# Retention of one mixer layer in two steps of four chunks instead of three steps of two

## The chip, the cores and the metric

The kernel runs on one core of one Trainium2 chip. The metric is the device time of one execution in microseconds (us). TensorE (PE in the profile) does the matrix products and writes them to PSUM; VectorE (DVE), ScalarE (ACT) and GpSimd (POOL) do the rest; SyncE (SP) only issues transfers.

## The reference, cut to what matters

The reference is a decoder trunk of two layers over 512 tokens of 1024 features. Each layer mixes with three parallel branches (RWKV-7, retention, a causal spatial gating unit, here "gating"), merges them with sigmoid gates, and follows with a gated MLP. The change is about the second and the third branch and about the merge:

```python
def retention_branch(p, cos, sin):            # 4 heads, 4 chunks of 128 tokens
    ...
    scores = jnp.einsum('bhnid,bhnjd->bhnij', qc, kc) * decay_in[:, None]
    inner = jnp.einsum('bhnij,bhnje->bhnie', scores, vc)
    kv = jnp.einsum('bhnjd,bhnje,hj->nbhde', kc, vc, k_dec).astype(jnp.float32)
    def step(R, kv_n):
        return R * chunk_decay + kv_n, R
    _, R_prev = lax.scan(step, jnp.zeros(...), kv)
    cross = jnp.einsum('bhnid,nbhde,hi->bhnie', qc, R_prev, q_dec)
    y = (inner + cross).transpose(0, 2, 3, 1, 4).reshape(B, S, RET_HEADS, RET_V_DIM)
    y = y * lax.rsqrt(jnp.mean(y * y, axis=-1, keepdims=True) + EPS)
    return (y.reshape(B, S, RET_V_WIDTH) * jax.nn.silu(g)).astype(p.dtype)

def sgu_branch(p, ln_g, ln_b, w_s, b_s):
    ...
    mixed = jnp.einsum('gij,bnjgd->bnigd', w, vc) + b_s.T[:, :, None]
    return u * mixed.reshape(B, S, SG_WIDTH)

proj = jnp.einsum('bsgc,gcd->bsgd', branches, w_branch[l])
x = x + jnp.sum(gates * proj, axis=2) @ w_out[l]
```

For each chunk n retention needs the scores of the chunk, a sum over the chunk for the state (`kv`), and a read-out: scores times values, plus the queries times the state that the earlier chunks left.

## The kernel before, in words

All large products are done in two halves of float32r: an operand is split into a high part (`hi`, or `sh`/`wh` for weights) and a low part (`lo`, `sl`/`wl`), and `mm3` (lines 153 to 163) issues three matmuls of 128 x 512 for each 128 x 128 block of weights. Weights come in units of 128 x 512: SP loads one (`wr`), ACT casts its high part (line 140), DVE subtracts the low part (line 141). `unit` (line 95) prepares them up to three units ahead in this stage, and the parts lie in a ring of 16 buffers (`r`), which also holds the turned queries and keys (`qF`, four buffers), the decayed keys (`kd`, three) and gating's normalised values (`sgv`, four). A second ring (`u`) has 31 buffers; the normalised input `h` takes 16 of them until the last product that reads it, the values and the gate of retention take 8, and scores (`sc`), states (`R`) and read-outs (`ry`) come from it too.

PSUM has eight banks in two pools of four: `acc` (line 78), where the large products add up, and `sm` (line 81), for everything small. A bank is handed on when the engine that reads it is done.

The code is emitted in one order and a planner orders the instructions of each engine at build time: by emission, but an instruction that is not ready in the planner's reckoning lets later ones pass. An instruction under `keep_in_program_order` is held behind the instruction emitted just before it on its engine. All of retention's and gating's small matmuls are held so; the matmuls of a merge are not.

The second half of the mixer (lines 420 to 458) is driven by the string `SEQ` (line 29), one letter or digit for a step, once for each of the two layers:

- `0`, `2`, `1`: one of eight blocks of a merge with branch 0 (RWKV), 2 (gating), 1 (retention): `merge`, line 1067. Twelve matmuls on one unit of weights into one `acc` bank; POOL issues the load of the block's gate (`gth`, line 1071); DVE multiplies gate and product (line 1074), which frees the bank; for branch 2 POOL, for branch 1 DVE adds to the sum (line 1077), and after branch 1 the sum is split.
- `U`: one of gating's two remaining up-projections (24 matmuls, one `acc` bank, freed by DVE at line 1040).
- `H`: `ret_heads` (line 922) reorders queries and keys on ACT and makes `kd` on DVE.
- `G`: `sgu_out` (line 1055), one of gating's four blocks: four matmuls into one `sm` bank, DVE reads it at line 1061.
- `S`: `ret_pair` (line 940) with the chunks to read out, to score and to sum. Its matmuls are emitted in this order: scores times values, queries times states, keys times queries (new scores), keys times values (sums for the states). Then ACT copies the read-outs out of PSUM (line 972), DVE masks the scores (line 976) and runs the states (lines 984 and 986), and the read-outs are normalised (lines 991 to 999): square on ACT, sum on DVE, power on POOL (line 996), product with the gate on DVE (line 999).
- `Y`: `ret_out` (line 1001) transposes the gated read-outs and splits them for the merge.

Before, `S` runs three times: scores of chunks 0 and 1 with all three sums; read-out of 0 and 1 with scores of 2 and 3; read-out of 2 and 3. Every `S` takes two `sm` banks for two chunks of read-outs, two for two chunks of scores, and the first takes two more for the sums.

The small matmuls are in plain float32, and each of them stands as two instructions in the trace.

Of the kernel before, what the change touches and what calls it, by code (L numbers as in the profile page):

```python
# [13 lines left out]
ADD, SUB, MUL, POW, MAX = ALU.add, ALU.subtract, ALU.mult, ALU.pow, ALU.max  # L14
# [3 lines left out]
S = 512  # L18
NC = 4
# [6 lines left out]
KEPT = 6  # L26
PRE = {(0, "f", 2): 0, (0, "f", 4): 1, (0, "f", 6): 2, (0, "f", 8): 3, (0, "d", 0): 4, (0, "d", 1): 5, (0, "d", 2): 6, (0, "d", 3): 7,
       (0, "d", 4): 8, (0, "d", 5): 9, (0, "d", 6): 10}
SEQ = "0 H G G 0 S 0 U U S G 0 G 0 0 S 2 2 Y 0 0 2 1 2 1 2 1 2 1 2 1 2 1 1 1"
NRAW = 3  # L30
AHEAD = {None: 2, "p": 4, "r": 3, "f": 3, "u": 5, "q": 4}
DEEP = 6
# [20 lines left out]
class Emit:  # L53
# [357 lines left out]
    def mixer(self, l, nst):  # L411
        self.pool = None
        with self.tc.tile_pool(name=f"rw{l}", bufs=1) as rp:
            self.rwp = rp
            self.filler = self.fillers(l)
            st = self.rwkv(l, nst)
        for _ in self.filler:
            pass
        self.rp = self.tc.tile_pool(name=f"ff{l}", bufs=NFP)
        self.fp = self.rp.__enter__()  # L420
        self.gup, self.bs, self.ws = self.f(n="gup"), self.f((128, 4, 128), n="bs"), self.f((128, 4, 128), n="ws")
        with self.tc.high_priority():
            self.nc.sync.dma_start(self.gup, self.a["gup"][l])
        self.nc.sync.dma_start(self.bs.rearrange("p g i -> p (g i)"), self.a["sgb"][l:l + 1, :].to_broadcast([128, 512]))
        self.nc.sync.dma_start(self.ws, self.a["sgw"][l])
        self.pool = "f"
        sg, out = self.sgu_v(l), self.rwkv_out(l, *st)
        self.nc.vector.tensor_tensor(self.ws, self.ws, self.c("le").unsqueeze(1).to_broadcast([128, 4, 128]), op=MUL)
        self.qk = []
        for c in range(NC):  # L430
            self.qk.append(self.f(n="qkT"))
            self.turned(self.qk[c], self.f(n="qkt"), self.ro[c], self.nc.gpsimd)
        self.wsp = self.split(self.ws.rearrange("p g i -> p (g i)"), self.f)
        for step in (sg, sg, out, sg, out, sg, None, out, sg, out, sg):
            next(step) if step else self.sgu_bias()
        yrw, ysg, mg, out, m2 = self.yrw, [], [], [], 0
        self.pool = "r"
        rest = self.sgu_u(l, range(2, 4))
        rows = iter([((), (0, 1), (0, 1, 2)), ((0, 1), (2, 3)), ((2, 3),)])
        for step in SEQ.split():  # L440
            if step == "S":
                self.ret_pair(*next(rows))
            elif step == "G":
                ysg.append(self.sgu_out(len(ysg)))
            elif step == "H":
                self.ret_heads()
            elif step == "U":
                next(rest), next(rest)
            elif step == "Y":
                yret = self.ret_out()  # L450
            elif step == "0":
                mg.append(self.merge(l, 0, len(mg), yrw))
            elif step == "2":
                mg[m2] = self.merge(l, 2, m2, ysg, mg[m2])
                m2 += 1
            else:
                out.append(self.split(self.merge(l, 1, len(out), yret, mg[len(out)], self.nc.vector), self.f))
        return out
# [481 lines left out]
    def ret_pair(self, read=(), score=(), state=()):  # L940


        nc, V, A, T, po = self.nc, self.nc.vector, self.nc.scalar, self.nc.tensor, self.tc.keep_in_program_order
        hv, hd = [slice(0, 64), slice(64, 128)], [(j, h) for j in range(2) for h in range(2)]
        X, Z = [[self.sm((128, 2, 2, 128)) for _ in range(2)] if cs else None for cs in (read, score)]

        def mm(o, lhsT, rhs, start, stop=True):
            po(T.matmul(o, lhsT, rhs, start=start, stop=stop, skip_group_check=True))  # L948

        for k, c in enumerate(read):  # L950
            for j, h in hd:
                i = 2 * j + h
                mm(X[h][:, k, j, :], self.sc[c][:, j, h, :], self.vt[c][:, 128 * i:128 * i + 128], k == j == 0, c == 0)
        for k, c in enumerate(read):
            for j, h in hd if c else ():
                mm(X[h][:, k, j, :], self.qF[c][hv[h], j, :], self.R[c][hv[h], j, :], False)
        for k, c in enumerate(score):
            for j, h in hd:
                mm(Z[h][:, k, j, :], self.kF[c][hv[h], j, :], self.qF[c][hv[h], j, :], k == j == 0)
        pks = []  # L960
        for c in state:
            if c % 2 == 0:
                pks.append(self.sm((128, 2, 2, 128)))
            for j, h in hd:
                i = 2 * j + h
                mm(pks[-1][hv[h], c % 2, j, :], self.kd[c][:, i, :], self.vt[c][:, 128 * i:128 * i + 128], c % 2 == j == 0)
        rm = self.c("rmask").rearrange("p (j h i) -> p j h i", h=2, i=128)
        ys = []
        for k, c in enumerate(read):
            ys.append(self.u((128, 2, 2, 128), n="ry"))  # L970
            for h in range(2):
                A.copy(ys[k][:, :, h, :], X[h][:, k])
        for k, c in enumerate(score):
            sc = self.u((128, 2, 2, 128), n="sc")
            for h in range(2):
                V.tensor_tensor(sc[:, :, h, :], Z[h][:, k], rm[:, :, h, :], op=MUL)
            self.sc[c] = sc
        for c in state:
            if c % 2 == 0:
                Rs = self.u((128, 2, 2, 128), n="R")  # L980
            pk, R, Rn = pks[c // 2][:, c % 2], self.R.get(c), Rs[:, c % 2]
            for j in range(2):
                if c == 0:
                    V.tensor_copy(Rn[:, j, :], pk[:, j, :])
                else:
                    V.scalar_tensor_tensor(Rn[:, j, :], R[:, j, :], self.c("rdec")[:, j:j + 1], pk[:, j, :], op0=MUL, op1=ADD)
            self.R[c + 1] = Rn
        for k, c in enumerate(read):
            y, g = ys[k].rearrange("p j h e -> p (j h) e"), self.yg[c]
            sq = self.u((128, 4, 128), n="rsq")  # L990
            A.activation(sq, y, AF.Square)
            ss = self.small((128, 4), "rss")
            V.tensor_reduce(ss, sq, axis=AX.X, op=ADD)
            V.tensor_scalar(ss, ss, 4.0 / 128, 4e-6, op0=MUL, op1=ADD)
            rr = self.small((128, 4), "rrr")
            nc.gpsimd.tensor_tensor(rr, ss, self.c("mhalf")[:, 0:4], op=POW)
            for i in range(4):
                o = g[:, 128 * i:128 * i + 128]
                V.scalar_tensor_tensor(o, y[:, i, :], rr[:, i:i + 1], o, op0=MUL, op1=MUL)
# [482 lines left out]
```

## Time and profile before

| what | value |
|---|---|
| median of 3 runs | 1692.36 us (1691.71 to 1693.19) |
| the profiled execution | 1690.56 us |
| its span, first to last instruction | 1688.9 us |
| granted TensorE clock | 0.999 |
| DVE busy | 1216.6 us (72%) |
| ACT busy | 793.7 us (47%) |
| POOL busy | 261.2 us (15%) |
| moved by DMA | 260.01 MB, mean 154 GB/s |

The profile page gives the busy time of each engine, the chain of work that ended last, and groups of instructions by line. Times in the trace's views are us from the start of the span. A matmul's row lasts longer than the distance to the next one, since matmuls are pipelined, so what PE takes is read from the distance between starts, not from the durations. The stage of the change lies between about 358 and 458 us in layer 0 and 844 us later in layer 1.

### The profile page before, as it was taken

Reading aid. Unit: us, or ns where it says so; the run is one execution under the profiler, and the core shown is the slowest. Engines: PE = TensorE matmul, PEld = TensorE weight load, DVE = VectorE, ACT = ScalarE, POOL = GpSimd, SP = SyncE. Lnnn points to the kernel's source line nnn. Section 1 sums busy time; section 2 is a strip of 40 time slices with the busy share of each in tenths; the row PEclk is TensorE's granted clock in tenths of the full one; section 3 lists DMA queues with packets and bytes.
Section 4 is the critical chain, followed back from the end, with each engine's and each line's share of the span. In section 5 each row is a group of like instructions: output and inputs, shape, how many; then the busy total and the mean of one; then the engine's idle time right before and its main releaser. Section 6 shows DMA issues by size and latency. Waiting matters only on the chain.

```text
span 1688.9 us, 27943 instructions
## 1 busy us (share of the span) xinstructions
PE 1680.4 (100%) x10247; PEld 1382.5 (82%) x10247; DVE 1216.6 (72%) x2115; ACT 793.7 (47%) x1365; POOL 261.2 (15%) x376
## 2 busy tenths in 40 slices
PE   9999999999999999999999999999999999999998
PEld 7888877888888888888888888778888888888887
DVE  7888745578669887655568888455786688887777
ACT  6563543554255444433346544335542544444555
POOL 1121000303301200003321210003032012220000
PEclk9999999999999999999999999999999999999999
DMA  5236553625544532147743265536254424443775
GB/s 183 88 110 207 178 176 96 189 85 171 184 150 144 194 124 94 62 146 264 251 146 97 91 208 186 176 99 187 86 173 157 156 94 144 144 141 113 245 241 177
DMA packets 143385, 260.01 MB, mean 154 GB/s; under 512 B 19440, under 2 KB 35440, under 8 KB 143248
## 3 DMA queue, kind: packets, MB, share of 16 engines
q1 hardware_dynamic: 117056, 188.41, 34.7%
q0 software_dynamic: 17552, 54.15, 9.7%
q10 hardware_dynamic: 8640, 15.67, 2.6%
q8 instruction: 80, 1.31, 0.3%
q14 instruction: 57, 0.47, 0.1%
HBM read 212.94 MB, written 45.22 MB: 153 GB/s over the span
## 4 chain that ended last, share of the span: by engine, by line
PE 98%; DVE 1%; ACT 0%; issue 0%; DMA 0%; DVEq 0%; ACTq 0%
PE acc L157 89%; PE sm L157 3%; PE sm L696 2%; PE sm L948 1%; PE sm L603 1%; PE sm L1059 0%; PE acc L359 0%; PE sm L566 0%; PE sm L565 0%; PE sm L1006 0%; DVE wl L141 0%; PE sm L850 0%; PE acc L319 0%; PE sm L841 0%; DMA wr<-wall 0%
## 5 line engine op out<-in xcount | busy, mean ns | idle before, releaser
L157 PE MATMUL acc<-lo,sh 128*128 128x512 f32 x1108 | 432.9, 391 | 0.0
L157 PE MATMUL acc<-hi,sh 128*128 128x512 f32 x1108 | 431.6, 390 | 0.0
L157 PE MATMUL acc<-hi,sl 128*128 128x512 f32 x1108 | 425.2, 390 | 0.0
L140 ACT CAST sh<-wr 128x512 fp32r<-128x512 f32 (+1 forms) x375 | 226.5, 614 | 305.3 <-PE acc L157 163.8
L141 DVE TENSOR_TENSOR sl<-wr,sh 128x512 fp32r<-128x512 f32 (+1 forms) x375 | 253.2, 684 | 95.9 <-ACT sh L140 71.5
L141 DVE TENSOR_TENSOR wl<-wr,wh 128x512 fp32r<-128x512 f32 x238 | 168.2, 710 | 139.9 <-ACT wh L140 136.0
L140 ACT CAST wh<-wr 128x512 fp32r<-128x512 f32 x238 | 146.8, 619 | 246.6 <-PE acc L157 166.2
L157 PEld LDWEIGHTS acc<-lo,sh 128*128 128x128 f32 x1108 | 208.1, 188 | 43.9 <-issue 0.9
L157 PEld LDWEIGHTS acc<-hi,sl 128*128 128x128 f32 x1108 | 208.1, 188 | 43.4 <-issue 0.2
L157 PEld LDWEIGHTS acc<-hi,sh 128*128 128x128 f32 x1108 | 208.2, 188 | 42.5
L157 PE MATMUL acc<-lo,wh 128*128 128x512 f32 x584 | 230.2, 394 | 0.0
L157 PE MATMUL acc<-hi,wl 128*128 128x512 f32 x584 | 228.2, 391 | 0.0
L157 PE MATMUL acc<-hi,wh 128*128 128x512 f32 x584 | 227.9, 390 | 0.0
L1125 ACT ACTIVATE cv<-fu,pc 128x512 f32<-128x512 f32 x88 | 71.7, 816 | 134.6 <-DVE fu L1123 134.6
L157 PEld LDWEIGHTS acc<-lo,wh 128*128 128x128 f32 x584 | 109.7, 188 | 23.7 <-DVE rwp L525 0.3
L157 PEld LDWEIGHTS acc<-hi,wl 128*128 128x128 f32 x584 | 109.7, 188 | 23.7 <-issue 0.9
L157 PEld LDWEIGHTS acc<-hi,wh 128*128 128x128 f32 x584 | 109.7, 188 | 22.2 <-issue 0.2
L157 PE MATMUL acc<-ah,sh 128*128 128x512 f32 x352 | 108.5, 389 | 0.0
L1126 DVE SCALAR_TENSOR_TENSOR cv<-fu,pc,cv 128x511 f32<-128x511 f32 x88 | 65.9, 750 | 34.5 <-ACT cv L1125 34.5
L157 PE MATMUL acc<-wl,hi 128*128 128x512 f32 x212 | 85.8, 405 | 0.0
L157 PE MATMUL acc<-wh,hi 128*128 128x512 f32 x212 | 82.6, 389 | 0.0
L157 PE MATMUL acc<-wh,lo 128*128 128x512 f32 x212 | 82.5, 389 | 0.0
(368 smaller groups left out, 2428.6 us busy)
## 6 DMA issues: line engine op xcount, KB each, us to landing
wr<-wall SPq DMA_DIRECT2D x480, 256.0 KB, 2.8
gd<-gth ACTq DMA_DIRECT2D x48, 256.0 KB, 3.2
gth<-gd POOLq DMA_DIRECT2D x48, 256.0 KB, 3.5
pre<-wdt POOLq DMA_DIRECT2D x44, 256.0 KB, 5.9
ts<-pre POOLq DMA_DIRECT2D x44, 256.0 KB, 2.6
wr<-ts SPq DMA_DIRECT2D x44, 256.0 KB, 3.9
wr<-wdn SPq DMA_DIRECT2D x40, 256.0 KB, 4.0
wr<-wdt SPq DMA_DIRECT2D x33, 256.0 KB, 4.0
```

The costliest lines, as they stand in the source:

```text
L140: self.kept(self.nc.scalar.copy(hi[:, :n], raw[:, :n]))
L141: self.kept(self.nc.vector.tensor_tensor(lo[:, :n], raw[:, :n], hi[:, :n], op=SUB))
L157: i = self.nc.tensor.matmul(*x, **y, **kw)
L603: i = T.matmul(pK[hv[1 - h], j, :], bk[hv[h], c, 1, :], x[hv[h], c, :], start=True, stop=True)
L696: po(T.matmul(o, l, r, start=start, stop=True, skip_group_check=True))
L948: po(T.matmul(o, lhsT, rhs, start=start, stop=stop, skip_group_check=True))
L1125: A.activation(t, u, AF.Identity, scale=self.p("cw2", j), bias=self.p("cb", j))
L1126: V.scalar_tensor_tensor(t[:, 1:], u[:, :511], self.p("cw1", j), t[:, 1:], op0=MUL, op1=ADD)
```

## The change

`S` is called twice. The first call makes the scores of all four chunks and the three sums; the second reads out all four chunks. So a call takes one `sm` bank for each chunk (the lists `X` and `Z` have as many banks as there are chunks, two chunks of one half of the heads in a bank), four in all. The sums for the states no longer lie in `sm` but in two `acc` banks. `SEQ` is written anew: gating's four blocks come as two pairs (the first ahead of everything, the second ahead of the read-outs), and the merges are spread in another way around them. Every matmul, every instruction of the other engines and every transfer is still there, with the same operands.

```diff
-SEQ = "0 H G G 0 S 0 U U S G 0 G 0 0 S 2 2 Y 0 0 2 1 2 1 2 1 2 1 2 1 2 1 1 1"
+SEQ = "G G 0 H 0 S 0 U U G G 0 S 0 0 2 2 0 2 Y 0 2 2 1 2 1 2 1 2 1 1 1 1 1"
...
-        rows = iter([((), (0, 1), (0, 1, 2)), ((0, 1), (2, 3)), ((2, 3),)])
+        rows = iter([((), range(NC), range(NC - 1)), (range(NC),)])
...
-        X, Z = [[self.sm((128, 2, 2, 128)) for _ in range(2)] if cs else None for cs in (read, score)]
+        X, Z = [[self.sm((128, 2, 2, 128)) for _ in cs] for cs in (read, score)]
...
-                mm(X[h][:, k, j, :], self.sc[c][:, j, h, :], self.vt[c][:, 128 * i:128 * i + 128], k == j == 0, c == 0)
+                mm(X[k // 2 * 2 + h][:, k % 2, j, :], self.sc[c][:, j, h, :], self.vt[c][:, 128 * i:128 * i + 128], k % 2 == j == 0, c == 0)
...
-                mm(X[h][:, k, j, :], self.qF[c][hv[h], j, :], self.R[c][hv[h], j, :], False)
+                mm(X[k // 2 * 2 + h][:, k % 2, j, :], self.qF[c][hv[h], j, :], self.R[c][hv[h], j, :], False)
...
-                mm(Z[h][:, k, j, :], self.kF[c][hv[h], j, :], self.qF[c][hv[h], j, :], k == j == 0)
+                mm(Z[k // 2 * 2 + h][:, k % 2, j, :], self.kF[c][hv[h], j, :], self.qF[c][hv[h], j, :], k % 2 == j == 0)
...
-                pks.append(self.sm((128, 2, 2, 128)))
+                pks.append(self.acc((128, 2, 2, 128)))
...
-                A.copy(ys[k][:, :, h, :], X[h][:, k])
+                A.copy(ys[k][:, :, h, :], X[k // 2 * 2 + h][:, k % 2])
...
-                V.tensor_tensor(sc[:, :, h, :], Z[h][:, k], rm[:, :, h, :], op=MUL)
+                V.tensor_tensor(sc[:, :, h, :], Z[k // 2 * 2 + h][:, k % 2], rm[:, :, h, :], op=MUL)
```

## The prediction

> **What bounds the kernel now.** I read the page's first and fourth part, then who waits for whom on PE, then the stage itself by windows, by the chain in order of time, and instruction by instruction.
>
> ```profile
> PE 1680.4 (100%) x10247; PEld 1382.5 (82%) x10247; DVE 1216.6 (72%) x2115; ACT 793.7 (47%) x1365; POOL 261.2 (15%) x376
> PE 98%; DVE 1%; ACT 0%; issue 0%; DMA 0%; DVEq 0%; ACTq 0%
> ```
> ```profile
> PE acc L359 <- DVE rst L356: 1.5, 1, 1.5
> PE sm L620 <- ACT Y L608: 0.4, 1, 0.4
> PE sm L696 <- DVE s L756: 0.4, 2, 0.2
> PE acc L157 <- DVE sl L141: 0.2, 1, 0.2
> ```
> PE is busy all the time and is 98% of the chain that ended last. The four rows are all that PE waits for in 1688.9 us: 1.5 + 0.4 + 0.4 + 0.2 = 2.5 us, none of it on a line of the stage that changes. So no wait can be taken away there. What can be won is distance between matmuls; what can be lost is a new wait.
>
> ```profile
> 370.00:380.00 10.00, 10.00 (x73) 8.44 (x74) 10.00 (x23) 4.58 (x8) 0.00 (x0) 1.00 0.37 110
> ```
> ```profile
> 357.97 9.52 PE acc L157 x42
> 367.49 1.78 PE sm L1059 x16
> 369.27 0.70 PE acc L157 x3
> 369.97 2.55 PE sm L948 x40
> 372.53 9.06 PE acc L157 x39
> ...
> 1216.73 9.06 PE acc L157 x39
> ```
> The window behind the first S shows PE at 10.00, and DVE (the third pair of numbers) at 10.00 as well: there VectorE is full, and it is the engine that frees the banks. The chain gives the pace of a large matmul, 9.52 / 42 = 0.2267 us. Its counts also tell what runs: 42 + 3 + 39 = 84 = 3 x 12 + 2 x 24, three merges (m0, m1, m2) and the two up-projections (U0, U1). The last row shows layer 1 doing the same, so every term below counts twice.
>
> **The change part by part.** *Work.* No instruction goes or comes on any engine, and no transfer; the gates' loads on POOL move with their merges. This term is 0.
>
> *Switches between large and small matmuls.* PE's rows in order of time:
>
> ```profile
> 369.58 0.40 PE L157 MATMUL acc<-hi,sl 128*128 128x512 f32 x1
> 369.90 1.16 PE L948 MATMUL sm<-qF 64*128 64x128 f32 x16
> 371.00 1.53 PE L948 MATMUL sm<-vt,kd 128*64 128x128 f32 x24
> 372.46 0.50 PE L157 MATMUL acc<-lo,sh 128*128 128x512 f32 x1
> 372.79 0.40 PE L157 MATMUL acc<-hi,sh 128*128 128x512 f32 x1
> ...
> 381.43 1.94 PE L948 MATMUL sm<-vt,sc 128*128 128x128 f32 x16
> 383.30 0.72 PE L948 MATMUL sm<-R,qF 64*128 64x128 f32 x8
> 383.85 1.06 PE L948 MATMUL sm<-qF 64*128 64x128 f32 x16
> 384.84 0.50 PE L157 MATMUL acc<-lo,sh 128*128 128x512 f32 x1
> ...
> 386.79 1.05 PE L1059 MATMUL sm<-ws,sgv 128*128 128x128 f32 x8
> 387.60 0.48 PE L157 MATMUL acc<-hi,sl 128*128 128x512 f32 x1
> 387.91 0.40 PE L157 MATMUL acc<-lo,sh 128*128 128x512 f32 x1
> ...
> 394.95 1.95 PE L948 MATMUL sm<-vt,sc 128*128 128x128 f32 x16
> 396.82 1.16 PE L948 MATMUL sm<-R,qF 64*128 64x128 f32 x16
> 397.92 0.50 PE L157 MATMUL acc<-lo,sh 128*128 128x512 f32 x1
> ```
> By starts, the three S take 2.56 (369.90 to 372.46), 3.41 (381.43 to 384.84) and 2.97 us (394.95 to 397.92), 8.94 in all. The new first S has the scores of both, 1.10 + 0.99 = 2.09, and the sums, 371.00 to 372.46 = 1.46: 3.55 us. The new second S has 1.87 twice (scores times values) and 0.55 + 1.10 (queries times states): 5.39. Sum 8.94 again. What goes is one change back to large matmuls: the first start after S comes 0.33 us after the one before it (372.46 to 372.79), against 0.2267, so 0.10 us. A second part I can only bound: the 16 rows of scores times values take 117 ns each (1.87 / 16), gating's 8 rows of the same shape 101 ns (386.79 to 387.60, 0.81); if the difference, 16 x 16 ns = 0.26 us, is a price per block, one of two goes, if not, nothing does. Gating goes from three bursts (16, 8, 8) to two of 16: one return less, 387.60 to 387.91 = 0.31, so 0.08 us; but a block in a pair costs 1.78 / 2 = 0.89 by the chain, alone 0.81, so the second pair costs 0.16 more. Together 0 to 0.3 us a layer; I take 0.2, near the one return that surely goes, so 0.4 us for both layers.
>
> *The states' sums in `acc` banks.* DVE's rows behind the first S:
>
> ```profile
> 372.88 1.42 DVE L976 TENSOR_TENSOR sc<-sm,con 128x256 f32<-128x256 f32 x4
> 374.80 0.49 DVE L984 COPY R<-sm 128x128 f32<-128x128 f32 x2
> 377.00 0.61 DVE L986 SCALAR_TENSOR_TENSOR R<-R,con,sm 128x128 f32<-128x128 f32 x2
> 377.51 0.69 DVE L1074 SCALAR_TENSOR_TENSOR gth<-gth,acc 128x512 f32<-128x512 f32 x1
> 378.97 0.70 DVE L1040 TENSOR_TENSOR sgu<-acc,rsF 128x512 f32<-128x512 f32 x1
> ```
> Up to S the new order is like the old one, so m0, m1, m2 and U0 have the four `acc` banks. The sums take m0's and m1's. Then U0's remaining 3 x 12 + 24 - 45 = 15 matmuls run, and U1 needs a bank: one of the sums' or m2's. PE gets there at 369.90 + 3.55 + 0.10 + 15 x 0.2267 = 376.95 us on the old time axis. DVE has eight masks instead of four, 2.84 us from 372.88; with the copies 0.49 and the first two state steps 0.61 the first sums' bank is free at 376.8 if DVE does nothing else. If it keeps its other work of this time in the old order, m2's bank is free at 377.51 + 0.69 + 1.42 = 379.6. So U1 waits from nothing to 379.6 - 376.95 = 2.65 us. Below nothing there is no gain, since U1 follows without a gap today. I take nothing: the planner may put a state step or m2's product ahead of masks, which no one needs before the second S, and the first bank then comes in time. Both ends are kept. Queued on DVE behind the longer block are weights' low parts (line 141), but they are made up to three units ahead, 3 x 2.72 = 8.2 us of matmuls, against 1.42 more. The `u` ring is nearly full too: 16 + 8 + four scores + two states = 30 of 31 buffers, until U1 lets `h` go. U0's result takes the last one, and U1's comes after `h`; the masks can wait only for gating's temporaries. I count nothing.
>
> *The read-outs of four chunks.* They have 6 merges between S and Y, 6 x 2.72 = 16.3 us, and three more that need no Y behind it. POOL's two rows and one of DVE bound what happens:
>
> ```profile
> 387.71 2.53 POOL L996 TENSOR_TENSOR rrr<-rss,con 128x4 f32<-128x4 f32 x2 [23.50 <-DVE rss L994]
> 390.19 2.71 POOL L1071 DMA_DIRECT2D gth<-gd  x5
> ```
> ```profile
> 395.04 0.69 DVE L1074 SCALAR_TENSOR_TENSOR gth<-gth,acc 128x512 f32<-128x512 f32 x1
> ```
> The next gates were issued only behind the two powers, 390.19 - 384.84 = 5.35 us after S, and the first product came 395.04 - 390.19 = 4.85 us later. If four powers stand there, 5.35 + 2.53 + 4.85 = 12.7 us pass, while four banks last 4 x 2.72 = 10.9: a gap of 1.8 us. It is nothing if the gates are issued ahead of the powers. I take nothing, since in the row five loads went together, some for merges emitted behind the next S: POOL's order is not tied to that of the steps.
>
> *Waits on `sm`.* Four banks at once for each S. The second pair of G waits for the masks, but U0 and U1 (39 matmuls, 8.8 us) stand between; the read-outs wait for line 1061 of that pair, with m3 (2.72 us) between, and for all masks and states, done long before.
>
> *The end.* Five merges with branch 1 stand last. DVE owes each a product, a sum and two low parts, four rows of 0.69 = 2.8 us, against 2.72 of matmuls: 5 x 0.04 = 0.2 us behind, while the next stage's first product has seven eighths of its work before it needs the last sum. Nothing.
>
> **Sum.** 1690.56 - 0.4 = 1690.2 us against the profiled execution (span 1688.9 and 1.66 around it); the median of before lies 1.8 us above that execution, so 1692.36 - 0.4 = 1692.0 us.
>
> **The rivals.**
>
> - *Slower: U1 waits for a bank.* Place: behind the first S, in both layers. Price: 2.65 us twice, less 0.4, so 1692.36 + 4.9 = 1697.3. It decides from the point at which both sums' banks and m2's are still held when U0 ends (376.95 here). For it: DVE is full in just that window, and today m2's product came at 377.51 though PE was done with m2 before 369.90. Against it: banks were plentiful then, so nothing asked for an earlier product. 0.17.
> - *Gates behind four powers.* 1.8 us twice, less 0.4: 1695.6. For it: the old order on POOL. Against it: m3's own load is emitted ahead of the powers now, and a product freed early takes the gap away. 0.10; it stands near the bound of what can be told apart, so I give it half to "same".
> - *The change doesn't do what it says.* The merges' matmuls are not held, and a burst that must wait for a bank is cut in pieces with merges between, each with a return of 0.10 us. Then the three or more bursts are there as before: 1692.4. 0.15.
> - *PE slows down with short waits.* Waits of 2.65 us in every layer could take the clock down: the 24 matmuls of U1 at half pace would cost 5.4 us more a layer, 1692.36 + 10.8 = 1703.2. The window row shows the granted clock 1.00 (third number from the end), and 0.999 is the mean of the span with all its small gaps, so 0.02. [...]
> - *Faster.* PE's waits sum to 2.5 us and lie elsewhere, so over 3.4 us could only come from a new plan of later stages: 1688. 0.03.
>
> **How the numbers follow.** My forecast, PE without a new wait, has 0.53: 1692.0 us. The measurement of this kernel can tell 0.2%, 3.4 us, from no change. Same: 0.53 + 0.15 + 0.05 = 0.73, and 0.03 of the first rival where its wait is under 1.9 us; slower: 0.14 + 0.05 + 0.02 = 0.21; faster 0.03. Range: below, 1690.3 is the forecast less the 0.2 us by which the saving can be larger (0.3 instead of 0.2 a layer) and the 1.48 us over which the three runs of before spread; above, 1697.3 takes in the first rival. The clock and the faster case stay outside, 0.05, with part of the rest.
>
> **What would show it.** Right: L948 in two pieces of 56 rows a layer in the chain, some 3.5 and 5.4 us, no row of waits on PE for L1074, L1040 or L986, DVE still near full behind the first S. Wrong: a hole in PE's starts before the second up-projection, with DVE masks running (first rival); `acc` starved 11 us behind the second S with POOL's loads late (second); pieces of L948 shorter than 56 (third). The forecast would be wrong as a whole if the planner moved work of later stages.

## The result, and the profile after

| | before | after |
|---|---|---|
| median (5 runs each) | 1692.31 us (1690.36 to 1693.19) | 1706.75 us (1704.34 to 1706.94) |
| profiled execution | 1690.56 us | 1705.52 us |
| its span | 1688.9 us | 1703.8 us |
| granted clock, mean | 0.999 | 0.997 |

The ratio is 1.0083 (95% interval 1.0068 to 1.0098): slower by 14.4 us, and outside the predicted range of 1690.3 to 1697.3. I had forecast no change. The same two lines of the page as before, busy time and the chain by engine:

```profile
PE 1685.5 (99%) x10247; PEld 1385.9 (81%) x10247; DVE 1216.3 (71%) x2115; ACT 793.8 (47%) x1365; POOL 263.9 (15%) x376
PE 94%; DVE 2%; ACT 2%; DMA 1%; issue 1%; ACTq 0%; DVEq 0%; SPq 0%
```
The counts are those of before, so no work was added. PE's busy time grew by 5.1 us all the same, which is a hint at the clock (0.997 in the mean against 0.999). PE's part of the chain fell from 98% to 94%; DVE's rose from 1% to 2%, ACT's from 0% to 2%, that of DMA from 0% to 1%. Who waits for whom on PE (us in total, times, longest):

```profile
PE acc L157 <- DVE gth L1074: 8.1, 2, 4.0
PE acc L359 <- DVE rst L356: 1.5, 1, 1.5
PE acc L157 <- DVE rwp L525: 1.0, 1, 1.0
```
The first row is new: twice, once in each layer, a large matmul waits 4.0 us for a product of line 1074. PE's and DVE's rows in order of time say which matmul and which product:

```profile
369.42 1.53 PE L948 MATMUL acc<-vt,kd 128*64 128x128 f32 x24
374.98 0.80 PE L157 MATMUL acc<-lo,sh 128*128 128x512 f32 x1 [4.03 <-DVE gth L1074]
375.57 0.63 PE L157 MATMUL acc<-hi,sh 128*128 128x512 f32 x1
376.00 0.63 PE L157 MATMUL acc<-hi,sl 128*128 128x512 f32 x1
...
378.08 0.39 PE L157 MATMUL acc<-hi,sh 128*128 128x512 f32 x1
```
```profile
370.00 1.41 DVE L976 TENSOR_TENSOR sc<-sm,con 128x256 f32<-128x256 f32 x4
371.32 0.68 DVE L150 TENSOR_TENSOR lo<-sgm,hi 128x512 fp32r<-128x512 f32 x1
371.93 1.41 DVE L976 TENSOR_TENSOR sc<-sm,con 128x256 f32<-128x256 f32 x4
373.25 0.47 DVE L984 COPY R<-acc 128x128 f32<-128x128 f32 x2
373.65 0.68 DVE L141 TENSOR_TENSOR sl<-wr,sh 128x512 fp32r<-128x512 f32 x1
374.25 0.68 DVE L1074 SCALAR_TENSOR_TENSOR gth<-gth,acc 128x512 f32<-128x512 f32 x1
```
The waiting matmul is the first of m2, behind the sums; before, m2 and part of U0 ran ahead of the sums. It waits until m0's product is done, and that product stands on DVE behind all eight masks, though PE was done with m0 long before. In the kernel before it stood at 367.64, ahead of the masks:

```profile
367.64 0.68 DVE L1074 SCALAR_TENSOR_TENSOR gth<-gth,acc 128x512 f32<-128x512 f32 x1
```
The starts show a second loss: 375.57, 376.00, then 0.43 us each up to 377.71, where 0.2267 is the pace of a large matmul. Six large matmuls behind the wait run at that pace in layer 0 and 13 in layer 1. The windows give the granted clock of that time (third number from the end):

```profile
371.19:374.60 3.41, 0.00 (x0) 0.00 (x0) 3.41 (x10) 0.42 (x1) 0.00 (x0) 1.00 0.75 292
374.61:378.01 3.40, 3.03 (x7) 2.45 (x8) 1.94 (x6) 0.00 (x0) 0.00 (x0) 0.50 0.23 77
378.02:381.42 3.40, 3.40 (x16) 2.77 (x16) 1.29 (x2) 0.62 (x1) 0.00 (x0) 1.00 0.05 16
1221.10:1224.50 3.40, 0.32 (x6) 0.08 (x2) 3.40 (x11) 0.73 (x2) 0.00 (x0) 1.00 0.88 334
1224.52:1227.92 3.40, 2.47 (x6) 1.99 (x7) 2.51 (x7) 0.00 (x0) 0.00 (x0) 0.50 0.27 85
1227.93:1231.33 3.40, 3.40 (x10) 2.63 (x9) 0.72 (x2) 0.35 (x1) 0.00 (x0) 0.50 0.00 0
1231.35:1234.75 3.40, 3.40 (x17) 2.77 (x16) 1.24 (x2) 0.87 (x2) 0.00 (x0) 1.00 0.28 77
```
PE did nothing in the first window and 0.32 us of work in the first one of layer 1. In the next one the clock is 0.50, and in layer 1 it stays at 0.50 for two windows.

**Where the time went.** For a ledger I took every distance between the starts of two matmuls in the 90 us from line 1051's row on: small matmuls with their whole distance, large ones with what is over 0.2267 us. The sum is all that is not a large matmul at full pace.

| us per layer | before, both layers | after, layer 0 | after, layer 1 |
|---|---|---|---|
| wait behind the sums | 0 | 4.10 | 4.10 |
| large matmuls at half pace | 0 | 1.40 | 2.77 |
| gating's rows (two pairs) | 3.32 | 3.85 | 3.86 |
| rows of the new scores | 2.08 | 2.49 | 2.49 |
| rows of the sums | 1.46 | 1.46 | 1.46 |
| read-outs (3.75 + 1.64; after 3.66 + 1.54) | 5.39 | 5.20 | 5.20 |
| `Y` | 1.50 | 1.66 | 1.66 |
| returns to large matmuls | 1.16 | 0.73 | 0.73 |
| line 1051 | 0.46 | 0.46 | 0.46 |
| sum | 15.36 | 21.36 | 22.73 |

That is 6.0 + 7.4 = 13.4 us. The profiled executions differ by 14.96; 1.30 of the rest lies before the stage, where PE's order is the same in both kernels (the profiled runs of the experiments begin the stage 0.5 to 2.9 us later than that of before), and 0.3 elsewhere.

### The profile page after: what moved, and what is told of

It reads as the page before. It is cut to its first block, busy times and chain, and to the rows that moved or that the text cites. A ratio compares the mean times of both kernels' runs of the same rounds, so it can differ in the third digit from the quotient of the medians.

```text
span 1703.8 us, 27968 instructions
## 1 busy us (share of the span) xinstructions
PE 1685.5 (99%) x10247; PEld 1385.9 (81%) x10247; DVE 1216.3 (71%) x2115; ACT 793.8 (47%) x1365; POOL 263.9 (15%) x376
## 4 chain that ended last, share of the span: by engine, by line
PE 94%; DVE 2%; ACT 2%; DMA 1%; issue 1%; ACTq 0%; DVEq 0%; SPq 0%
PE acc L157 86%; PE sm L157 3%; PE sm L696 2%; PE sm L948 1%; PE sm L603 1%; DMA wua<-wua 0%; PE sm L1059 0%; DMA wr<-wk 0%; DVE sc L976 0%; DMA x<-xT 0%; ACT yF L780 0%; ACT wh L140 0%; DVE lo L150 0%; DVE sl L141 0%; PE sm L566 0%
```

## The experiments

The theory at the start, **T1, banks**: `acc` banks are handed out in the order of emission, not in the order in which PE runs. The emission is m0, m1, S, m2, U0; so the sums in `acc` take the third and fourth bank, m2 must take m0's and U0 m1's, and they can no longer pass S. How long they wait is set by where DVE does those products. Rivals: **T2, gating first** (the pair ahead of everything brings S too early) and **T3, masks** (eight masks at once are too much for DVE, wherever the sums lie). All results, with the ledger's sum for each layer:

| kernel | median, us | ratio to before, 95% interval | ledger, layers 0 and 1 |
|---|---|---|---|
| before | 1691.8 to 1692.3 | | 15.36, 15.36 |
| after | 1706.75 | 1.0083 [1.0068, 1.0098] | 21.36, 22.73 |
| sums_sm | 1693.99 | 1.0012 [1.0003, 1.0021] | 16.18, 16.18 |
| g_back | 1699.82 | 1.0045 [1.0031, 1.0059] | 18.83, 18.97 |
| g_first3 | 1696.37 | 1.0025 [1.0016, 1.0034] | 17.53, 17.50 |
| gates_early | 1694.07 | 1.0015 [1.0006, 1.0024] | 16.19, 16.16 |
| gates_early_gback | 1694.67 | 1.0018 [1.0009, 1.0026] | 16.57, 16.27 |
| gates_before | 1700.65 | 1.0048 [1.0035, 1.0061] | 18.58, 19.22 |
| sums_thrice | 1702.16 | 1.0058 [1.0045, 1.0071] | 18.97, 18.92 |
| sums_twice | 1701.85 | 1.0057 [1.0042, 1.0073] | 18.98, 18.97 |
| m2_ahead | 1706.33 | 1.0084 [1.0071, 1.0097] | 22.58, 21.82 |
| states_first | 1696.05 | 1.0025 [1.0014, 1.0036] | 17.45, 17.48 |
| sums_sm_gback | 1693.15 | 1.0009 [1.0000, 1.0017] | 15.75, 15.75 |

**sums_sm**: the kernel after with the sums back in `sm`.

```diff
-                pks.append(self.acc((128, 2, 2, 128)))
+                pks.append(self.sm((128, 2, 2, 128)))
```


> The changed kernel, with the sums for the states back in the small banks. Theory 1 (banks): acc banks are handed out in the order of emission, the sums take the third and fourth, so the third merge m2 must take m0's, and m0's product stands behind eight masks on VectorE. Then with the sums elsewhere m2 and the first up-projection run ahead of S again, PE's wait on line 1074 (8.1 us in two times) goes, and so does the half clock behind it: 1691 to 1695 us (the sums now wait for masks to free a bank, so up to 2 us may come back). Theory 2 (gating's pair ahead of everything brings S too early): nothing changes, 1704 to 1707. Theory 3 (eight masks in a row are too much for VectorE wherever the sums lie): 1702 to 1707.

1693.99 us, where before had 1692.16 in the same session: of the 14.4 us, 12.6 are gone, and PE has no wait for line 1074 at all. The chain in order of time shows m2 and part of U0 ahead of the small matmuls of S again (45 large ones between 358.89 and 370.50, as before):

```profile
358.89 8.18 PE acc L157 x36
...
370.50 1.09 PE sm L948 x16
```
The eight masks and gating's pair are both still there, so neither of the rivals makes the loss alone: it needs the sums in `acc`.

**g_back**: the kernel after with the first gating pair put back behind `H`.

```diff
-SEQ = "G G 0 H 0 S 0 U U G G 0 S 0 0 2 2 0 2 Y 0 2 2 1 2 1 2 1 2 1 1 1 1 1"
+SEQ = "0 H G G 0 S 0 U U G G 0 S 0 0 2 2 0 2 Y 0 2 2 1 2 1 2 1 2 1 1 1 1 1"
```


> The changed kernel, with the head of the order as before (0 H G G 0 S), so gating's first pair stands behind the first merge again. Theory 1 (banks): the sums still take the third and fourth acc bank ahead of m2, PE still waits some 4 us a layer: 1703 to 1707 us. Theory 2 (gating's pair first): the wait goes, 1691 to 1693. Theory 3 (masks): 1703 to 1707.

1699.82: neither. Half of the loss stays. PE's waits:

```profile
PE acc L157 <- DVE gth L1074: 3.4, 2, 1.7
PE acc L157 <- DVE lo L150: 1.8, 2, 0.9
```
Here m0's product stands at 366.81, ahead of the masks, and m2 has its bank; U0 waits 1.7 us for m1's, at 375.71 behind them. Of the 3.5 us a layer that the ledger has over before, 1.7 are this wait and 0.9 the one for a low part. The clock stays whole (1.00 in the stretch 1222.13:1225.53 of layer 1, 0.999 in the mean). So the gating pair matters too, where T1 as I wrote it gave it no part.

**g_first3**: the kernel before, three steps with the sums in `sm`, with the gating pair first.

```diff
-SEQ = "0 H G G 0 S 0 U U S G 0 G 0 0 S 2 2 Y 0 0 2 1 2 1 2 1 2 1 2 1 2 1 1 1"
+SEQ = "G G 0 H 0 S 0 U U S G 0 G 0 0 S 2 2 Y 0 0 2 1 2 1 2 1 2 1 2 1 2 1 1 1"
```


> The kernel before (three steps of retention, sums in small banks) with nothing but the new head of the order: G G 0 H 0 S. Theory 1 (banks): m2 and the first up-projection have the third and fourth acc bank, no new wait, 1691 to 1693.5 us. Theory 2: S comes too early and PE waits as in the changed kernel, 1700 to 1707. Theory 3 (masks, four here): as theory 1.

1696.37, where T1 promised no loss: a miss. m0's product moves to 380.06, behind the masks and the first state steps, and PE waits for it:

```profile
380.90 0.47 PE L157 MATMUL acc<-lo,sh 128*128 128x512 f32 x1 [1.59 <-DVE gth L1074]
```
With the sums in `sm` this reaches a later unit only and costs 2.2 us a layer. In the ledger of layer 0: neither edit 15.4; gating first alone (in three steps) 17.5; two steps with the sums in `acc`, without gating first, 18.8; both 21.4, of which 1.4 is the half pace that neither has alone. T1 needs this addition: the banks say who waits, and gating first moves the products that are waited for. With two steps and the sums in `sm` the same gating first costs only 0.4 a layer (16.18 in sums_sm against 15.75 in sums_sm_gback) and no wait: m0's product stands behind all eight masks there too (377.48, done at 378.17), but U1, the next unit that needs a bank, is behind the sums and starts at 378.58. So it hurts where the next unit asks for a bank earlier.

**gates_early**: the kernel after, with the gates of m0 and m1 loaded ahead of the stage.

```diff
+        self.ahead = [(0, m) for m in range(2)]
+        self.early = [self.f(n="gth") for _ in self.ahead]
+        for t, i in zip(self.early, self.ahead):
+            self.nc.gpsimd.dma_start(t, self.gd[i])
...
-        t = self.f(n="gth")
-        nc.gpsimd.dma_start(t, self.gd[br, m])
+        t = self.early.pop(0) if self.early else self.f(n="gth")
+        if (br, m) not in self.ahead:
+            nc.gpsimd.dma_start(t, self.gd[br, m])
```


> The changed kernel, but the gates of the first two merges are loaded ahead of the stage, so that their products can stand ahead of the eight masks on VectorE; banks, order string and all else as in the changed kernel. Theory 1 (banks): m0's and m1's banks are free when S ends, m2 starts right behind S, PE waits under 1 us in all there: 1690.5 to 1693 us, and the saving on switches (0 to 0.6 us) can be seen at last. Theory 2: 1704 to 1707. Theory 3 (VectorE is full with eight masks): the products are earlier but weights' low parts come late, 1697 to 1704.

1694.07, and the wait is gone with the sums still in `acc`; the saving on switches that I expected besides (1690.5 to 1693) does not show. DVE's rows (line numbers are 4 or 5 higher):

```profile
364.89 0.68 DVE L1079 SCALAR_TENSOR_TENSOR gth<-gth,acc 128x512 f32<-128x512 f32 x1
...
366.15 0.68 DVE L1079 SCALAR_TENSOR_TENSOR gth<-gth,acc 128x512 f32<-128x512 f32 x1
...
369.27 0.75 DVE L980 TENSOR_TENSOR sc<-sm,con 128x256 f32<-128x256 f32 x2
```
Both products stand ahead of the masks. So it was the load of the gate, as the planner reckons it, that held the product back. On the chip the product of the kernel after did not wait for its gate: the first of ten gate loads was issued at 363.78, none took over 6.0 us to land, and the product stands at 374.25 with no idle time in front of it. So the order is one of build time.

**m2_ahead**: the kernel after with m2 named ahead of the first `S`.

```diff
-SEQ = "G G 0 H 0 S 0 U U G G 0 S 0 0 2 2 0 2 Y 0 2 2 1 2 1 2 1 2 1 1 1 1 1"
+SEQ = "G G 0 H 0 0 S U U G G 0 S 0 0 2 2 0 2 Y 0 2 2 1 2 1 2 1 2 1 1 1 1 1"
```


> The kernel after with the third merge m2 named ahead of the first S, so that it takes the third accumulator bank and the sums take the fourth and m0's. Banks by emission order: m2 runs ahead of S as in the kernel before; the wait on the products L1074 moves to the sums themselves (L948) or to U0, and is shorter, since some 2 us of m2's matmuls now lie in front: 1695 to 1702, and no half clock if the wait is under 2 us. Rival, that m2 waits for its gates or its weights whatever bank it has: the wait stays on L157 and the time within 2 us of 1706.75.

The place was right, the size was not: 1706.33. PE's rows:

```profile
371.14 1.09 PE L948 MATMUL acc<-vt,kd 128*64 128x128 f32 x16
377.31 1.12 PE L948 MATMUL acc<-vt,kd 128*64 128x128 f32 x8 [5.07 <-DVE gth L1074]
```
The sums themselves now wait, for the same product. Since m2's matmuls run first, S and its masks come 1.7 us later (371.72 instead of 370.00) and the product behind them with it (376.57 instead of 374.25); the wait isn't shorter but longer. This shows directly that a tile's turn for a bank goes by emission: only the order of emission was changed, and another tile waits for m0.

**states_first**: the kernel after with the loop of the masks moved below that of the states.

```diff
-        for k, c in enumerate(score):
-            sc = self.u((128, 2, 2, 128), n="sc")
-            ...
         for c in state:
             ...
+        for k, c in enumerate(score):
+            sc = self.u((128, 2, 2, 128), n="sc")
+            ...
```

> The kernel after with the states' instructions on DVE ahead of the eight masks; the planner then puts m0's product behind the first steps of the states, and m1's behind all masks. If what PE waits for is nothing but the place of m0's product on DVE: m2's wait is 2 to 3 us in each layer instead of 4.03, no half rate, U0 perhaps waits up to 2 us for m1's; 1700 to 1704. Rival, that something else (the second tile of the sums being in use, a weight) ends the wait: it stays near 4 us and 1705 to 1707.

1696.05, below the range expected. The wait ends earlier, and U0 doesn't wait. PE's rows, then DVE's:

```profile
369.62 1.53 PE L948 MATMUL acc<-vt,kd 128*64 128x128 f32 x24
372.72 0.47 PE L157 MATMUL acc<-lo,sh 128*128 128x512 f32 x1 [1.57 <-DVE R L981]
```
```profile
371.98 0.60 DVE L981 SCALAR_TENSOR_TENSOR R<-R,con,acc 128x128 f32<-128x128 f32 x2
372.49 0.68 DVE L1074 SCALAR_TENSOR_TENSOR gth<-gth,acc 128x512 f32<-128x512 f32 x1
```
The trace names the state's row as releaser, and it must be that one: m2's first matmul starts at 372.72, while m0's product ends only at 373.17. So m2 has the bank of the first two sums here and not m0's, against what I expected and against T1's wording that m2 "must take m0's". A tile's turn comes by emission, but the bank that it gets is, as far as these runs show, the one that comes free first: m0's in the kernel after, the sums' here. That also explains U0: its matmuls follow without a gap, ahead of m1's product at 376.26. DVE's order sets the end of the wait: 4.03 became 1.57 us though nothing on PE was changed.

**sums_twice and sums_thrice**: the sums of the states computed two or three times over, into the same banks. The diff is that of sums_thrice; sums_twice has `range(1)`.

```diff
+        for _ in range(2):
+            for c in state:
+                for j, h in hd:
+                    i = 2 * j + h
+                    mm(pks[c // 2][hv[h], c % 2, j, :], self.kd[c][:, i, :], self.vt[c][:, 128 * i:128 * i + 128], c % 2 == j == 0)
```


> The kernel after with the sums for the states computed twice over (24 more matmuls per layer, about 1.5 us of PE work in each, 3 in all). If a wait has to reach some length before the matmuls behind it run at half rate, and that length lies between 1.8 and 4.0 us: wait on L1074's line about 0.8 to 2.5 us in each layer, no matmul 428 ns from the next, 1700 to 1703. If any wait behind the sums costs it in proportion: some half-rate matmuls stay, 1703 to 1706.

> The kernel after with the sums for the states computed three times over (same result; 48 more matmuls of 64 ns each over two layers, about 2.9 us of PE work per layer, 5.8 in all). If the slow matmuls behind the 4.03 us wait come of the length of PE's idleness, the wait gets shorter by the added work (about 1 to 2 us left), no matmul stands 428 ns from the next, the clock of the stretch is 0.97 and more, and the added work costs next to nothing on balance: wait + work stay about the same and the half rate (1.4 and 2.6 us in the two layers) goes: 1700 to 1704. Rival, that the slow matmuls come of something else in that stretch (the reads of the banks, the DMA traffic of 283 to 318 GB/s beside it): the half rate stays, and 1705.5 to 1711.

Both have more work than the kernel after, and are faster: 1701.85 and 1702.16. First sums_twice, then sums_thrice, PE's rows:

```profile
370.86 2.84 PE L948 MATMUL acc<-vt,kd 128*64 128x128 f32 x48
...
375.42 0.50 PE L157 MATMUL acc<-lo,sh 128*128 128x512 f32 x1 [1.73 <-DVE gth L1079]
```
```profile
370.52 4.15 PE L948 MATMUL acc<-vt,kd 128*64 128x128 f32 x72
375.09 0.50 PE L157 MATMUL acc<-lo,sh 128*128 128x512 f32 x1 [0.42 <-DVE gth L1079]
```
From the first sum to m2's first matmul it is 4.57 us in both, by starts (375.42 - 370.86 = 4.56, 375.09 - 370.52 = 4.57): the end of the wait is set by DVE, and the work put into the hole was free here. In the kernel after it is 5.56; the missing 1.0 us is a new place of the product, right behind the masks instead of behind the copies of the states and a weight's low part (374.36 in sums_thrice, whose stage begins 1.1 us later). No large matmul runs at 0.43 us, and the clock is 1.00. In sums_twice DVE is busy in all of the 3.40 us from 1220.49 to 1223.89 and the transfers move 337 GB/s there, as much as beside the wait in the kernel after (292 and 334). So in these runs the half pace went with PE's wait (4.03 us in the kernel after, 1.73 and 0.42 here), not with DVE's work or the transfers beside it. The ledgers explain 7.2 us of the 9.9 (sums_twice) and 10.4 (sums_thrice) by which these two are above before; another 2.7 and 2.4 us stand before the stage in their profiled runs, and I have no cause for that.

**gates_early_gback and gates_before**: the early gates together with the order of g_back; and the early gates alone in the kernel before.

> The kernel after with both remedies: the gates of the first two merges loaded ahead of the stage, and the first gating pair put back behind H, so that m0's and m1's products stand ahead of the eight masks and the pair's matmuls lie in one burst. Banks by emission order (the theory that holds so far): no wait on the products L1074, the granted clock whole, the gating rows back to their 3.32 us per layer, and only the saved switches left: about 0.65 us per layer under the kernel before, 1690.5 to 1692, ratio 0.999 to 1.000. Rival, that G behind H brings S to meet the products whatever the gates do: 1698 to 1701, as with the pair alone put back (1699.82).

1694.67, better than g_back but no better than the early gates alone. No wait on the products is left, but a large matmul now waits up to 1.2 us for its low part (line 150), and the gain expected of fewer switches does not come: 16.57 and 16.27 in the ledger against 15.36. (Its profiled execution took 1698.65 us, 4.0 above the median; outside the stage, PE waits 2.0 us at line 700 in layer 1 there, and the clock is 0.50 behind it, in 1106.49:1109.88.)

> Control: the kernel before with the gates of the first two merges loaded ahead of the stage. If the early gates only undo what the new order does to the products, nothing changes: 1691.5 to 1693, ratio 0.9995 to 1.0005. Rival, that the gates held something in the kernel before as well: under 1691.3, ratio under 0.9993.

This control missed widely: 1700.65. In layers 0 and 1, behind `Y`:

```profile
421.95 0.50 PE L157 MATMUL acc<-lo,sh 128*128 128x512 f32 x1 [2.90 <-DVE gth L1079]
...
1269.86 0.62 PE L157 MATMUL acc<-lo,sh 128*128 128x512 f32 x1 [1.90 <-DVE gth L1079]
```
The product stands behind a weight's low part (420.60), which had waited 3.75 us for the high part, and that 4.46 us for the weight's transfer. So two loads moved ahead have shifted the order of a stage 50 us later. Why that transfer came late I did not follow up.

**sums_sm_gback**: the two steps of four chunks and the second gating pair alone: sums in `sm`, first gating pair behind `H` (the diffs of sums_sm and g_back).

> The kernel after with the sums in sm's banks and the first gating pair put back behind H: what stays of the change is the merging of the chunks into two steps and the second gating pair. Both ingredients of the wait are gone: no wait on the products, clock 1.00, and in layer 0 the switches saved behind Y (about 0.2 us each layer in the read-outs): 1691 to 1693, ratio 0.9990 to 1.0005. Rival, that eight masks at once or four read-outs at once cost something of their own wherever the sums lie: 1693.5 to 1696.

1693.15, ratio 1.0009 [1.0000, 1.0017]: just above what I expected. No new wait, clock whole (0.999 in the mean). The ledger has +0.39 us a layer: new scores +0.31 (cut in pieces of 18 and 14 rows), `Y` +0.16, gating +0.08, read-outs -0.19, returns 0. No version here beats the kernel before.

## Why the prediction was wrong, step by step

- **What bounds the kernel** was right: PE, with no wait in the stage, so a change could only lose by a new wait. It did.
- **Work: 0.** Right, the counts are equal.
- **The states' sums in `acc` banks: the step that failed.** It began: "Up to S the new order is like the old one, so m0, m1, m2 and U0 have the four `acc` banks. The sums take m0's and m1's." That is the order in which PE ran before, not the one in which banks are handed out. In the string, `S` stands ahead of m2 and `U` in the old order too; they passed it only because the sums lay in `sm`. With the sums in `acc` the third and fourth bank are theirs (m2_ahead and sums_sm show it), so it is m2 that needs m0's bank, not U1 that needs the sums'. I had put the second wait at 0 to 2.65 us and took 0; the real one is 4.03. The rest of my argument, "the planner may put a state step or m2's product ahead of masks", asked for the right thing of the wrong tile, and the planner did not do it: m0's product stood behind all masks. My picture that a tile gets whichever of several banks comes free first was right (states_first); who would be asking, and when, was not.
- **Gating's pair first** I had looked at only for its switches. That it moves m0's product behind the masks (g_first3: 2.2 us a layer with nothing else changed) was in no step.
- **Switches: -0.2 us a layer.** The returns gave more than that, -0.43, and the read-outs -0.19. But other rows took back more. Gating has +0.53: its first pair is cut in three, and the large matmul behind the second piece waits 0.20 us for its low part (line 150). The new scores have +0.41: they pause at 368.03 until DVE has read a bank of gating (line 1061, done at 368.27). `Y` has +0.16, for which I have no cause. The net is +0.5, not -0.2 (gates_early and sums_sm, without the wait, have +0.8 in all). "I count nothing" for waits on `sm` looked at the second pair only; the first one is where they are.
- **Read-outs of four chunks, and the end.** No wait of PE there, as forecast; the powers on POOL did not hold the gates.
- **The rivals.** The first, a wait for a bank behind the first S with DVE full of masks, had the right place and kind, though another tile and a price of 2.65 instead of 4.1 us. The clock rival had 24 matmuls at half pace, 5.4 us a layer; it came with 6 and 13, for 1.4 and 2.8 us. I gave it 0.02 because the mean clock of before was 0.999; but that kernel has no wait over 1.5 us, so its clock says nothing of longer ones. I also treated the two as one or the other, while here the wait of 4.03 us brought the half pace along in both layers: 4.1 + 1.4 and 4.1 + 2.8 us a layer are both of them.

## What to carry to other kernels

When a tile moves to another pool, write down the order in which that pool's buffers are handed out, by emission, and for each later tile which earlier ones could free a buffer for it and which instruction does so first; the order in which the engine ran before says nothing about it. Then ask of each freeing instruction where it stands in its engine's queue, in particular whether something emitted ahead of it (here eight masks) is in front. A wait of PE is priced with its length and with what the clock does behind it: here these were 4.10 us, and 1.40 and 2.77 for the two layers. Work put into the hole told the two apart (sums_thrice: a wait of 0.42 us, clock 1.00).

## What the runs showed of the chip that I had not expected

In these runs the granted clock fell to 0.50 behind some waits, and the length of a wait alone does not say behind which. In the trace of the kernel after it falls from 1.00 to 0.50 at 374.60 and 1224.51 and is back at 378.01 and 1231.34: 3.41 us at half in layer 0 and 6.83 in layer 1, behind a wait of 4.03 us in both. Beside the wait's own length this cost 1.40 and 2.77 us of pace. Stretches around the waits in gates_before (layer 0 in the first row, layer 1 in the others), and in m2_ahead:

```profile
420.17:423.58 3.41, 1.63 (x7) 1.37 (x8) 2.98 (x5) 0.92 (x2) 0.00 (x0) 1.00 0.28 82
1266.68:1270.08 3.40, 1.50 (x7) 0.97 (x6) 1.52 (x3) 1.24 (x2) 0.00 (x0) 1.00 0.45 174
1270.10:1273.49 3.39, 3.39 (x9) 2.64 (x9) 3.29 (x5) 0.00 (x0) 1.66 (x2) 0.50 0.47 155
```
```profile
372.10:375.50 3.40, 0.14 (x4) 0.00 (x0) 3.40 (x10) 0.87 (x2) 0.00 (x0) 1.00 0.64 246
375.52:378.92 3.40, 1.61 (x9) 1.23 (x10) 3.40 (x10) 0.44 (x1) 0.00 (x0) 0.50 0.25 77
378.93:382.33 3.40, 3.40 (x9) 2.63 (x8) 0.55 (x3) 0.17 (x1) 0.00 (x0) 0.50 0.00 1
```
In m2_ahead the clock is 0.50 from within the wait of 5.07 us on. In gates_before it is 0.50 behind the wait of 1.90 us in layer 1, but stays at 1.00 around the longer one of 2.90 us in layer 0, and the large matmuls behind that one follow at 0.23 us. In gates_early_gback it is 0.50 behind the wait of 2.0 us. The waits of 1.57 to 1.73 us in states_first, g_back and sums_twice cost only their length. The expectations of m2_ahead (2 us) and sums_twice (between 1.8 and 4.0 us) supposed one length of wait from which on the clock falls; that was an estimate, and no run shows such a length. What decides between 1.90 us with the loss and 2.90 us without it was not shown.
